# Streaming encoder trunk: the modulation's matmul groups of the first feed-forward, joined two by two

## The chip, the cores and the metric

The kernel runs on one core of a Trainium2 chip, in one launch. The core has five engines that work side by side, each from its own queue of instructions in a fixed order: TensorE (PE in the profile; its weight loads are listed apart as PEld), VectorE (DVE), ScalarE (ACT), GpSimd (POOL), and SyncE (SP), which here does nothing but issue DMA transfers. They wait for one another by semaphores. The metric is the device time of the whole launch in microseconds; lower is better.

## The reference, cut to what matters

An encoder with two layers works on 1024 prompt positions and 8 x 16 sample positions, 1152 rows of 1024 numbers in all. Every sub-layer is modulated by a conditioning vector `c`, of which there are nine (one for the prompt, eight for the samples):

```python
sc = jax.nn.silu(c)
for l in range(DEPTH):
    ada = (sc @ w_ada[l] + b_ada[l])[:, None, :]
    sh_m, sc_m, g_m, sh_f, sc_f, g_f = jnp.split(ada, 6, axis=-1)
    h = x * (1 + sc_m) + sh_m
    ...                                   # attention of the layer
    x = layer_norm(DEEPNORM_ALPHA * x + (1 + g_m) * mix, ...)
    h = x * (1 + sc_f) + sh_f
    f, conv_rows = conv_ffn(h, ..., w_up[l], conv_w[l], conv_b[l], w_down[l])
    x = layer_norm(DEEPNORM_ALPHA * x + (1 + g_f) * f, ...)
    if l == N_A_LAYERS - 1:
        ada_kv = (sc @ w_ada_kv + b_ada_kv)[:, None, :]
        ...                               # the K/V that the second layer uses
```

`conv_ffn` multiplies by `w_up` (1024 x 5632), runs a causal convolution of width 3 over the positions, gates one half by the other through a GELU, and multiplies by `w_down` (2816 x 1024). The modulation `sc @ w` is a product of nine rows with 1024 x 2048 numbers, seven times in all. It is small work, but its weights are 8 MB each time.

## The kernel before, in words

**Two streams of work.** TensorE does nearly everything that takes time. The modulation is computed beside it, in the background: `ada(gi, bank, ring)` (line 220) is a generator, and `step(n)` (line 200) pulls it on by one piece. Seven such pieces of modulation exist (`gi` 0 to 6). `gi` 0 is made in the opening, 1 and 2 run beside the first attention, and 3, 4, 5 and 6 run beside the first feed-forward: line 1422 queues them as `self.bg`.

**One modulation.** 1024 x 2048 weights come as 16 loads of 512 KB (line 229), for `k` of 0 to 7 (128 rows of the contraction) and `hf` of 0 and 1 (half of the columns). Each load feeds four matmuls (line 237): `cT`, 32 columns wide (nine used), is the stationary operand, and the array is used as four column tiles of 32, one per `j`, each with its own 256 moving columns. The type is fp32, for which every matmul leaves two records in the profile, so that one load's group is 8 records. All groups add up in one bank of PSUM (bank 7). Then a last piece adds the bias (`adab`, line 253), forms a gate row for two of the four (`gd`), turns the row with four transposes (line 264) and copies it to `adaT`. After each load's group, and after the last piece, the generator yields. `issue_after` ties a matmul behind another one in TensorE's queue; with `high_priority` this keeps the four matmuls of a load together.

**The first feed-forward.** The 22 column blocks of the gate's two halves are taken as pairs `j`. Pairs 0 and 1 are plain. Pairs 2 to 21 (`spair`, line 1389) use a scheme with seven products of half the size instead of eight (`products`, line 1154): the block of `w_up` for the one half is loaded into `sa`, that for the other into `sg`; GpSimd forms the sums S1, S2, S3 and `a21` from them (lines 1174 to 1177), each is split into a high and a low part (`split`, ScalarE then VectorE), and TensorE runs the products 11, 2, 21, 3, 1, 4, 22 in this order (pair 2: 11, 21, 22, 2, 3, 1, 4). Each is 24 matmuls (line 1226), 12 of 320 columns and 12 of 256. Product 11 and product 21 need only `sa`; product 2 needs S2, product 1 needs S1, and S1 = `a21` + `a22` is made of `sg`. Every product is read out of PSUM by `evict` before the next one adds to the same bank. The calls of line 1399 pull the background on by one piece after the first, third, fifth and seventh product: four groups of modulation per pair.

**The ring of slots.** `sa`, `sg`, every modulation load and the bias row all take the next slot of one ring of four, `wide` (line 1267): two slots of `ws` and two in `F`. A pair takes six of them, so a slot is reused four requests later, and a load can start only when the last reader of that slot is done. Line 1429 takes one more slot after pair 2 for `tables_b`, a small table; when that table is in `eb`, `skew_b` (line 1794) copies 384 KB of it in DRAM for each of 16 heads. These copies are written at pairs 3 to 18, but nothing ties them there but SyncE's queue.

**What sets the order.** The queues' orders are written by a planner when the program is built: it goes through the program with estimated times, and on each engine takes the instruction that stands first in the program among those that are ready by then. So a group of modulation can be moved a little ahead or back, and SyncE's queue can hold a copy ahead of a load that comes earlier in the program but whose slot was still taken.

Of the kernel before, what the change touches and what calls it, by code (L numbers as in the profile page):

```python
# [105 lines left out]
class Trunk:  # L106
# [110 lines left out]
                pass  # L217


    def ada(self, gi, bank, ring=None):  # L220

        nc = self.nc
        ring = ring or self.ws
        ps = self.bank(bank)
        lead = [None] * 4
        for k in range(8):
            for hf in range(2):
                w = ring.next()
                nc.sync.dma_start(w, self.I["adaw"][gi, k, hf])
                for j in range(4):  # L230
                    with ExitStack() as es:
                        if lead[j] is not None:
                            es.enter_context(self.tc.issue_after(lead[j]))
                        if j:
                            es.enter_context(self.tc.high_priority())
                            es.enter_context(self.tc.issue_after(first))
                        mm = nc.tensor.matmul(
                            ps[32 * j : 32 * j + 32, hf * 256 : hf * 256 + 256],
                            self.cT[:, k * 32 : k * 32 + 32],
                            w[:, j * 256 : j * 256 + 256],  # L240
                            start=k == 0 and hf == 0,
                            stop=k == 7 and hf == 1,
                            tile_position=(0, 32 * j),
                            skip_group_check=True,
                        )
                    first = mm.ins if j == 0 else first
                    lead[j] = lead[j] or mm.ins
                yield
        row = ring.next()
        bsrc = self.I["adab"][gi : gi + 1, :]  # L250
        for j in range(4):
            nc.sync.dma_start(
                row[32 * j : 32 * j + 32, 512:1024].rearrange("p (h x) -> p h x", h=2),
                bass.AP(bsrc.tensor, bsrc.offset + j * 256, [[0, 32], [1024, 2], [1, 256]]),
            )
        nc.vector.tensor_add(row[:, 0:512], ps, row[:, 512:1024])
        gate = {1: (0, 0), 2: (1, 1), 5: (2, 0), 6: (3, 1)}.get(gi)
        if gate is not None:
            g, hf = gate
            nc.gpsimd.tensor_scalar_add(row[:, 512:768], row[:, hf * 256 : hf * 256 + 256], 1.0)  # L260
            for j in range(4):
                nc.sync.dma_start(self.gd[g, :, j * 256 : j * 256 + 256], row[32 * j : 32 * j + 9, 512:768])
        for i in range(4):
            nc.tensor.transpose(ps[:, i * 128 : i * 128 + 128], row[:, i * 128 : i * 128 + 128], self.ident)
        dst = self.adaT[:, gi * 144 : gi * 144 + 144].rearrange("p (h j i r) -> p h i j r", h=2, j=4, i=2)
        src = ps.rearrange("p (h i j r) -> p h i j r", h=2, i=2, j=4)
        for h in range(2):
            nc.vector.tensor_copy(dst[:, h], src[:, h, :, :, 0:9])
        yield
# [971 lines left out]
    def ffn(self, l, xsrc, xdst, affs):  # L1241
        nc, I, O, H, F = self.nc, self.I, self.O, self.H, self.F
# [11 lines left out]
        g = nc.gpsimd  # L1254
# [12 lines left out]
        wide = Ring(self.ws.items + [F[:, 11644:12668], F[:, 8700:9724]])  # L1267
# [76 lines left out]
        def gated(j, ya, yg):  # L1344
            nc.scalar.activation(yg, yg, AF.Gelu_apprx_tanh)
            nc.gpsimd.tensor_mul(yg, yg, ya)  # L1346
            if l == 0 or j % 2:
                nc.sync.dma_start(self.actD[j], yg)
                if l:
                    self.pend.append(j // 2)  # L1350
            else:
                for r in (slice(0, 512), slice(1024, 1152)):
                    nc.sync.dma_start(self.actD[j][:, r], yg[:, r])

        def act_sums():
            for m in self.pend:
                a11, a21 = ygate[0][:, 0:512], ygate[0][:, 512:1024]
                a12, a22 = ygate[1][:, 0:512], ygate[1][:, 512:1024]
                nc.gpsimd.tensor_add(a22, a21, a22)
                nc.gpsimd.tensor_sub(a21, a11, a21)  # L1360
                nc.gpsimd.tensor_sub(a11, a22, a11)
                nc.gpsimd.tensor_sub(a12, a12, a11)
                for i in range(2):
                    nc.sync.dma_start(self.actS[m, i], ygate[i][:, 0:1024])
            self.pend = []

        def weight_sums(m):
            b11, b12, b21, b22 = (t[:, o : o + 512] for t in self.w0 for o in (0, 512))
            for i in range(2):
                nc.sync.dma_start(self.w0[i], I["wdn"][l, 2 * m + i])  # L1370
            nc.gpsimd.tensor_sub(b12, b22, b12)
            nc.gpsimd.tensor_add(b22, b12, b11)
            nc.gpsimd.tensor_sub(b21, b22, b21)
            nc.sync.dma_start(self.wT[m, 0][:, 512:1024], b12)
            nc.sync.dma_start(self.wT[m, 1], self.w0[1])
# [13 lines left out]
        def spair(j):  # L1389
            sa, sg = self.ws.next(), self.ws.next()  # L1390
            nc.sync.dma_start(sa, I["wup"][l, j])
            pairdma = nc.sync.dma_start(sg, I["wup"][l, j + 22]).ins
            ua, ug = us.next(), us.next()
            y = []
            row = conv_row_psum if l else conv_row

            def after(i, q):
                if i % 2 == 0:
                    self.step(1)
                if l and i == 1:  # L1400
                    act_sums()
                if l and i == 2 and j in wsum:
                    with self.tc.issue_after(pairdma):
                        weight_sums(wsum.index(j))
                if q == 4:
                    y.append(ygate[j % 2] if l else ys.next())
                    row(ug, j, 1, y[0])

            self.products(sa, sg, ua, ug, (S1, S2, S3), p1s, sub, TT, after, "first" if j == NPL else None)
            ya = yact if l else ys.next()  # L1410
            row(ua, j, 0, ya)
            gated(j, ya, y[0])
# [6 lines left out]
            self.take_w0(F32)  # L1419
        self.ws = wide  # L1420
        if l == 0:
            self.bg = [self.ada(g, 7, wide) for g in (3, 4, 5, 6)]
        self.tsums(Ring([F[:, 1536:2560], F[:, 8700:9724], F[:, 11644:12668]]), (0, 1, 2, 3, 4, 8, 5, 6, 7), T1S, TT)
        for u in us.items:
            nc.gpsimd.memset(u[:, 0:2], 0.0)
# [631 lines left out]
```

## Time and profile before

| what | value |
|---|---|
| time, median of 3 runs | 2776.96 us (2775.85 to 2781.15) |
| the profiled execution's own time | 2778.73 us |
| its span, first to last instruction | 2776.9 us |
| TensorE busy | 2656.2 us (96%) |
| VectorE, ScalarE, GpSimd busy | 69%, 49%, 38% |
| DMA queue of SyncE, share of 16 engines | 54.6% |
| pairs 2 to 21 of the first feed-forward on TensorE | 532.3 to 1036.1 us of the span |
| modulation groups of that stretch | 547.0 to 961.2 us, 512 records |

In the profile each line of an order of time has its start in us from the span's start, its length, engine, line of the kernel, operation, what it writes and reads, its shape and how many instructions were merged into it. Behind them, in brackets, stands how long the engine had stood idle before and what ended that. A busy TensorE is an engine with records on it; matmuls overlap, so that lengths can't be added, and distances from start to start are what counts.

### The profile page before, as it was taken

To read this page: it belongs to the slowest core of one execution; us is meant where nothing else is said; L and a number is where in the kernel's file an instruction comes from. 1 tells how busy PE (TensorE), PEld (TensorE's weight loads), DVE (VectorE), ACT (ScalarE), POOL (GpSimd) and SP (SyncE) were. 2 spreads that over 40 slices of the span, in tenths; PEclk is the share of its full clock that TensorE was granted. 3 is DMA by queue.
4 is the path that set the end of the run, shared out by engine and by line. 5 is a ranking of instruction groups with operands and counts; after the bars stand their busy time and mean duration, and the time that the engine had idled before them with its cause. 6 is when DMAs were issued, how large, how long until landed. Compare 5 with 4: busy or idle time off the path is not lost.

```text
span 2776.9 us, 47111 instructions
## 1 busy us (share of the span) xinstructions
PE 2656.2 (96%) x17266; PEld 2345.9 (84%) x17266; DVE 1916.0 (69%) x3836; ACT 1348.0 (49%) x2777; POOL 1065.7 (38%) x775
## 2 busy tenths in 40 slices
PE   7999889999999999999999999989999999999997
PEld 5987768989999998888898888867899999997776
DVE  4376767776666684767754667766787777785669
ACT  3475723433334343443536666662454445454454
POOL 3132623444434357664220121242466656632101
PEclk9999999999999999999999999989999999999999
DMA  7756434464444446765757457773544443347564
GB/s 289 236 162 193 145 103 167 163 236 148 139 158 147 147 135 220 240 217 182 277 192 263 121 155 195 213 213 115 176 143 173 144 138 135 136 148 246 189 221 155
DMA packets 229527, 498.27 MB, mean 179 GB/s; under 512 B 37456, under 2 KB 99232, under 8 KB 229296
## 3 DMA queue, kind: packets, MB, share of 16 engines
q1 hardware_dynamic: 229296, 495.27, 54.6%
q8 instruction: 136, 2.23, 0.3%
q14 instruction: 95, 0.78, 0.1%
HBM read 378.15 MB, written 126.47 MB: 182 GB/s over the span
## 4 chain that ended last, share of the span: by engine, by line
PE 38%; DVE 6%; DMA 4%; ACT 2%; issue 1%; POOL 0%; SPq 0%; DVEq 0%; ACTq 0%; POOLq 0%
PE PS L1226 18%; PE PS L1600 5%; PE PS L322 5%; PE PS L309 4%; PE PS L605 2%; PE PS L583 2%; DMA xa<-actD 1%; PE PS L554 1%; DVE xa L191 1%; DVE F L521 1%; DVE wl L191 1%; PE PS L557 1%; DMA xa<-actS 1%; PE PS L732 0%; DMA wl<-wT 0%
## 5 line engine op out<-in xcount | busy, mean ns | idle before, releaser
L1226 PE MATMUL PS<-H,wh 128*128 128x256 f32 (+1 forms) x2288 | 355.8, 296 | 0.0
L1187 DVE TENSOR_TENSOR F<-PS,F 128x256 f32<-128x256 f32 (+1 forms) x446 | 197.9, 453 | 182.1 <-PE PS L1226 172.7
L1226 PEld LDWEIGHTS PS<-H,wh 128*128 128x128 f32 x2288 | 322.6, 190 | 0.4 <-issue 0.4
L180 ACT CAST wh<-F 128x512 fp32r<-128x512 f32 (+3 forms) x241 | 147.7, 624 | 212.5 <-PE PS L1226 105.5
L191 DVE TENSOR_TENSOR wl<-F,wh 128x512 fp32r<-128x512 f32 (+2 forms) x225 | 213.4, 960 | 40.6 <-ACT wh L180 38.4
L1226 PE MATMUL PS<-H,wl 128*128 128x256 f32 (+1 forms) x1144 | 202.0, 297 | 6.2 <-ACT F L1194 6.2
L1600 PE MATMUL PS<-wh,xa 128*128 128x512 f32 x584 | 187.8, 398 | 14.6 <-ACT wh L180 7.6
L1226 PEld LDWEIGHTS PS<-H,wl 128*128 128x128 f32 x1144 | 168.6, 189 | 12.1 <-ACT F L1194 6.4
L1226 PE MATMUL PS<-xa,wh 128*128 128x320 f32 (+1 forms) x1152 | 175.2, 293 | 0.0
L180 ACT CAST xa<-xa 128x384 fp32r<-128x384 f32 (+2 forms) x143 | 85.8, 604 | 176.0 <-DMA xa<-actD 149.6
L1226 PEld LDWEIGHTS PS<-xa,wh 128*128 128x128 f32 x1152 | 159.0, 188 | 0.4 <-issue 0.4
L1469 DVE TENSOR_TENSOR xa<-xa 128x384 fp32r<-128x384 f32 x66 | 94.4, 1441 | 83.4 <-ACT xa L180 83.3
L1600 PEld LDWEIGHTS PS<-wh,xa 128*128 128x128 f32 x584 | 110.3, 190 | 44.3 <-ACT wh L180 11.8
L180 ACT CAST wh<-ws 128x512 fp32r<-128x512 f32 (+1 forms) x131 | 95.5, 736 | 101.4 <-PE PS L1226 44.2
L643 POOL TENSOR_TENSOR F<-F,x2r 64x512 f32<-64x512 f32 x62 | 79.4, 1280 | 165.9 <-DVE F L619 149.3
L1346 POOL TENSOR_TENSOR F<-F 128x1152 f32<-128x1152 f32 x44 | 124.1, 2820 | 43.9 <-DVE F L1339 18.1
L322 PE MATMUL PS<-xa,H 128*128 128x512 f32 x504 | 133.5, 406 | 6.2 <-ACT xa L180 3.3
L309 PE MATMUL PS<-H,w0r 128*128 128x384 f32 (+1 forms) x720 | 136.1, 340 | 0.0
L1275 DVE SCALAR_TENSOR_TENSOR F<-F 128x1024 f32<-128x1024 f32 (+2 forms) x160 | 132.1, 876 | 3.1 <-ACT F L1314 2.1
L309 PE MATMUL PS<-H,wh 128*128 128x384 f32 (+1 forms) x672 | 131.1, 338 | 0.0
L583 PE MATMUL PS<-C,F 128*128 128x128 f32 x720 | 112.7, 281 | 14.5 <-DVE wh L590 5.8
L309 PEld LDWEIGHTS PS<-H,w0r 128*128 128x128 f32 x720 | 123.2, 188 | 2.8 <-issue 1.1
(354 smaller groups left out, 6883.8 us busy)
## 6 DMA issues: line engine op xcount, KB each, us to landing
ws<-in_adaw_dram SPq DMA_DIRECT2D x64, 512.0 KB
ws<-in_wup_dram SPq DMA_DIRECT2D x49, 512.0 KB
F<-in_adaw_dram SPq DMA_DIRECT2D x48, 512.0 KB
F<-in_wup_dram SPq DMA_DIRECT2D x39, 512.0 KB
actD<-F SPq DMA_DIRECT2D x33, 576.0 KB
ws<-in_wdn_dram SPq DMA_DIRECT2D x33, 512.0 KB
F<-in_wdn_dram SPq DMA_DIRECT2D x33, 512.0 KB
xa<-kH SPq DMA_DIRECT2D x60, 256.0 KB
```

The source lines that it names most:

```text
L180: nc.scalar.copy(out, in_)
L191: self.eng(el).tensor_sub(lo, src, hi.bitcast(F32))
L309: mm = self.nc.tensor.matmul(out[:, 0:n], w[a][:, k * 128 : k * 128 + 128], H[:, p, k, s0 : s0 + n], start=i == 0, stop=i == 23)
L322: self.nc.tensor.matmul(out[:, 0:n], H[:, p, j * kn + k, t0 : t0 + 128], w[a][:, k * n : k * n + n], start=i == 0, stop=i == 23,)
L583: nc.tensor.transpose(t[:, n * 128 : n * 128 + 128], p[:, (kt - k0) * 128 : (kt - k0) * 128 + 128], self.ident)
L643: self.eng("v" if last else "p").tensor_mul(on[r, q], on[r, q], rb[r, :])
L1187: nc.vector.tensor_add(d, v(ps), a if len(a.shape) == 3 else v(a))
L1226: self.pairmm = nc.tensor.matmul(ps[:, 0:m], w[a][:, k * 128 : k * 128 + 128], x(p, k, n), start=start and c == 0, stop=c == 11, skip_grou ...
L1275: nc.vector.scalar_tensor_tensor(o, u, cw[:, cc, i : i + 1], o, op0=ALU.mult, op1=ALU.add)
L1346: nc.gpsimd.tensor_mul(yg, yg, ya)
L1469: nc.vector.tensor_sub(lo, raw, hi.bitcast(F32))
L1600: self.downmm = nc.tensor.matmul(ps, a[p][:, i * 128 : i * 128 + 128], w[q], start=first and c == 0, stop=last and c == 2, skip_group_chec ...
```

## The change

`ada` gets a parameter `per`, the number of loads that make one piece. With `per` of 1 it does what it did before, and so it stays beside the first attention. Beside the first feed-forward `per` is 2: a piece issues the loads of `hf` 0 and 1 of one `k`, then the matmuls of `hf` 1, then those of `hf` 0, and all but the first of these eight matmuls are tied behind the first at high priority. The generator has nine pieces instead of seventeen. They are pulled on after the third and the seventh product of a pair, and no longer after the first, third, fifth and seventh. Four modulations are then 36 pieces in 18 pairs; before they were 68 pieces in 17 pairs.

```diff
-    def ada(self, gi, bank, ring=None):
+    def ada(self, gi, bank, ring=None, per=1):
...
-        for k in range(8):
-            for hf in range(2):
-                w = ring.next()
-                nc.sync.dma_start(w, self.I["adaw"][gi, k, hf])
+        order = [(k, hf) for k in range(8) for hf in range(2)]
+        for o in range(0, 16, per):
+            loads = []
+            for k, hf in order[o : o + per]:
+                loads.append(ring.next())
+                nc.sync.dma_start(loads[-1], self.I["adaw"][gi, k, hf])
+            first = None
+            for (k, hf), w in reversed(list(zip(order[o : o + per], loads))):
                 for j in range(4):
                     with ExitStack() as es:
                         if lead[j] is not None:
                             es.enter_context(self.tc.issue_after(lead[j]))
-                        if j:
+                        if first is not None:
                             es.enter_context(self.tc.high_priority())
                             es.enter_context(self.tc.issue_after(first))
...
-                            start=k == 0 and hf == 0,
-                            stop=k == 7 and hf == 1,
+                            start=o == 0 and lead[j] is None,
+                            stop=o + per == 16 and hf == (0 if per > 1 else 1),
...
-                    first = mm.ins if j == 0 else first
+                    first = first or mm.ins
                     lead[j] = lead[j] or mm.ins
-                yield
+            yield
...
             def after(i, q):
-                if i % 2 == 0:
+                if i in (2, 6):
                     self.step(1)
...
-            self.bg = [self.ada(g, 7, wide) for g in (3, 4, 5, 6)]
+            self.bg = [self.ada(g, 7, wide, 2) for g in (3, 4, 5, 6)]
```

## The prediction

> **What bounds the kernel now.** I read the page first, then the first feed-forward by stretches, then TensorE's order of work there, then the queue that issues the loads.
>
> ```profile
> span 2776.9 us, 47111 instructions
> PE 2656.2 (96%) x17266; PEld 2345.9 (84%) x17266; DVE 1916.0 (69%) x3836; ACT 1348.0 (49%) x2777; POOL 1065.7 (38%) x775
> ```
>
> ```profile
> 532.30:561.10 28.80, 26.38 (x202) 24.33 (x200) 19.95 (x38) 12.27 (x23) 10.63 (x11) 0.94 0.52 162
> 561.10:616.80 55.70, 50.80 (x405) 46.40 (x402) 40.88 (x54) 19.93 (x35) 21.43 (x15) 1.00 0.72 251
> 616.80:968.50 351.70, 351.70 (x2786) 323.34 (x2785) 234.28 (x362) 133.78 (x225) 143.45 (x108) 1.00 0.44 146
> 968.50:1036.10 67.60, 67.00 (x507) 66.75 (x506) 56.94 (x77) 32.52 (x53) 36.31 (x23) 1.00 0.39 127
> ```
>
> The stretches (columns: PE, PEld, DVE, ACT, POOL busy, then clock, DMA share, GB/s) are pair 2; pairs 3 and 4; pairs 5 to 18; and 19 to 21. From pair 5 on TensorE is busy for 351.70 of 351.70 us at a granted clock of 1.00, DVE for two thirds of it and the DMA engines for 0.44. There only TensorE's own time counts, so a shorter record stream is time won. Pairs 3 and 4 are another stage: 4.9 us of TensorE idle, DMA at 0.72.
>
> **What a switch to the modulation's records costs.** TensorE's order of time, in four places: a period of four groups, seven products without any group, and the two places where two groups already stand together.
>
> ```profile
> 546.44 0.60 PE L1226 MATMUL PS<-xa,wh 128*128 128x320 f32 x3
> 546.98 1.07 PE L237 MATMUL PS<-F,C 128*32 128x256 f32 x16
> 547.98 1.00 PE L1226 MATMUL PS<-xa,wh 128*128 128x320 f32 x5
> ...
> 576.56 0.64 PE L237 MATMUL PS<-ws,C 128*32 128x256 f32 x8 [1.77 <-DMA ws<-in_adaw_dram]
> 577.02 0.61 PE L237 MATMUL PS<-F,C 128*32 128x256 f32 x8
> 577.56 1.29 PE L1226 MATMUL PS<-H,wh 128*128 128x320 f32 x7
> ...
> 720.50 0.64 PE L237 MATMUL PS<-ws,C 128*32 128x256 f32 x8
> 721.07 0.85 PE L1226 MATMUL PS<-xa,wl 128*128 128x320 f32 x4
> ...
> 745.68 0.64 PE L237 MATMUL PS<-F,C 128*32 128x256 f32 x8
> ...
> 978.16 0.75 PE L1226 MATMUL PS<-xa,wl 128*128 128x320 f32 x4
> ...
> 1000.31 0.75 PE L1226 MATMUL PS<-H,wl 128*128 128x320 f32 x4
> ```
>
> Seven products take 1000.31 - 978.16 = 22.15 us (3.16 each). The same seven with four groups take 745.68 - 720.50 = 25.18. So a group of eight records costs (25.18 - 22.15) / 4 = 0.76 us. Only 0.57 of it (721.07 - 720.50) lies from its first record to the next product; the other 0.19 is lost to the products at its two edges, as the first four records behind it show (0.85 against the usual 0.75). Sixteen records together take 547.98 - 546.98 = 1.00 and 577.56 - 576.56 = 1.00: the second eight add 0.43. Joining two groups therefore saves 0.76 - 0.43 = 0.33 us.
>
> ```profile
> L237 PE MATMUL PS<-ws,C 128*32 128x256 f32 x208 | 16.6, 391 | 0.0
> L237 PE MATMUL PS<-F,C 128*32 128x256 f32 x208 | 16.6, 391 | 0.0
> ```
>
> Pairs 5 to 18 hold 416 records, 52 groups, which become 26: **26 x 0.33 = 8.6 us less**. Nothing else is removed: the same 64 loads, the same records. The bounds: if the two joined rows above are flattered by their places, and a join saves only one of the two edges, half of it, 4.3; upwards, the whole stretch has (351.7 - 14 x 22.15) / 52 = 0.80 per group, three closing rows included, and 26 x 0.37 makes 9.6. I take 8.6, since both joined rows agree to 0.01.
>
> A rule speaks against this. The Trainium skill, page "TensorE: Matmul & The Clock Gate", Part 3, "What overlaps and what doesn't", says that a weight load overlaps running matmuls only where the row group differs; these tiles differ by column only. By it the second eight records would show their eight weight loads in the open; by the joined rows of this trace (0.43 us for the second eight) they do not.
>
> **What the move does to the loads.** Products go by their names here (P11, P2, P21, P3, P1, P4, P22, in this order within a pair) and their places by first to seventh. In pairs 5 to 18 the ring of four slots mostly works out so: a pair's own two weight loads (`sa`, `sg`) reuse the slots of the first two modulation loads of the pair before. Today these are free after its first and its third product, in the change both after the third; `sa` is issued some 7 us later (now 721.21, then beside 728.31) and `sg` a few tenths later.
>
> ```profile
> 717.26 0.33 SPq L229 DMA_DIRECT2D F<-in_adaw_dram  x1
> 721.21 0.33 SPq L1391 DMA_DIRECT2D ws<-in_wup_dram  x1
> 725.27 0.33 SPq L1348 DMA_DIRECT2D actD<-F  x1
> 728.31 0.33 SPq L1392 DMA_DIRECT2D F<-in_wup_dram  x1
> ```
>
> ```profile
> 731.79 1.29 POOL L1174 TENSOR_TENSOR F<-F 128x512 f32<-128x512 f32 x1 [6.54 <-DMA F<-in_wup_dram]
> 733.04 1.29 POOL L1176 TENSOR_TENSOR F<-ws,F 128x512 f32<-128x512 f32 x1
> ```
>
> A load takes 3.5 us (728.31 to the sum that waited for it, 731.79). Two behind each other: some 5.5. `S2` (line 1176) is then there 2 us later than now, at 736.3. P2, which needs it, is the second product of the next pair: this pair starts one product before the group at 720.50, at 717.3, the next some 24.5 us later, its P2 at 745. That cover of nearly 9 us, less 3 for the split, holds. What queues behind the two loads on SyncE is the `actD` store and the next modulation loads; POOL waits 2 us longer at `S1` (it idles 6.54 there), and nothing but the `actD` store waits for it. The two loads of the group behind the third product are issued at the pair's start, when the last group of the pair before frees their slots, and have 3 x 3.16 = 9.5 us for 5.5. So I cost the steady pairs at nothing; without that cover each missing microsecond comes 14 times.
>
> **The one place where the slot counts: pair 3.** Line 1429 takes one slot after pair 2, so pair 3's `sg` reuses the slot of pair 2's third modulation load. Its records run at 550.27 now; in the change they come behind the seventh product, with the fourth load's, at 560.54.
>
> ```profile
> 550.27 0.64 PE L237 MATMUL PS<-ws,C 128*32 128x256 f32 x8
> ...
> 560.54 0.64 PE L237 MATMUL PS<-ws,C 128*32 128x256 f32 x8
> 561.11 0.85 PE L1226 MATMUL PS<-H,wl 128*128 128x320 f32 x4
> ...
> 619.85 0.64 PE L237 MATMUL PS<-ws,C 128*32 128x256 f32 x8
> ```
>
> ```profile
> 551.00 0.59 SPq L1392 DMA_DIRECT2D ws<-in_wup_dram  x1
> 554.00 0.33 SPq L229 DMA_DIRECT2D F<-in_adaw_dram  x1
> 554.39 8.59 SPq L1794 DMA_DIRECT2D skb<-eb  x10
> ...
> 566.16 0.33 SPq L229 DMA_DIRECT2D ws<-in_adaw_dram  x1
> ...
> 571.05 3.82 SPq L1794 DMA_DIRECT2D skb<-eb  x3
> ...
> 577.72 0.39 SPq L1392 DMA_DIRECT2D F<-in_wup_dram  x1
> ```
>
> ```profile
> 555.26 1.30 POOL L1174 TENSOR_TENSOR F<-ws 128x512 f32<-128x512 f32 x1 [6.48 <-DMA ws<-in_wup_dram]
> ...
> 588.61 1.26 POOL L1174 TENSOR_TENSOR F<-F 128x512 f32<-128x512 f32 x1 [14.72 <-DMA F<-in_wup_dram]
> ```
>
> ```profile
> 558.29 1.77 DVE L191 TENSOR_TENSOR wl<-F,wh 128x512 fp32r<-128x512 f32 x1
> ```
>
> Today that load goes out at 551.00, ahead of the sixteen copies of line 1794, and lands in 4.3 us (555.26). In the change it is free at about 561 and goes out behind some ten copies, at about 563. Its flight there is between 4.3 us and the 10.4 of the load at 566.16 (its records start at 576.56) or 10.9 (577.72 to 588.61); I take 8.5, nearer the crowded rows: it lands at 571.5. From landing to the end of `S2`'s split took 560.06 - 555.26 = 4.8, so P2 can start at 576.3. P11 and P21 need `sa` alone; they fill 560.8 (561.11 less 0.33) to 567.1. TensorE then idles up to 9.2 us, and some 2.6 less if P1, which needs only `S1` (one POOL sum and the wait for it earlier, 1.3 each), goes first. I take 8.
>
> Pair 5 starts one product before 619.85, at 616.7. In the change it starts at 560.8 + 14 products (44.3) + four joined groups (4 x 1.19 = 4.8) + 8 = 617.9: **1.2 us more**. The present waits in that stretch (4.9 us) are gone in this count, since they too were for loads that the new stall lets land.
>
> **Sum:** -8.6 + 1.2 = -7.4 us. The profiled execution took 2778.73 us, 1.8 above its span and 1.8 above the median shown (2776.96). 2778.73 - 7.4 = 2771.3; against the median, **2769.5**.
>
> **Rivals.**
> (a) *Pair 3 is not held up*: the planner puts pair 2's last sixteen records early (it used one group to fill a gap at 550.27), or the load ahead of the copies. For it: 550.27 was such a gap. Against: in the change P1 stands before them in the program and has no wait there. Pair 5 then starts at 609.9 plus the 1.8 us wait of 576.56, 611.7: -5.0 - 8.6 = -13.6, 2763.4.
> (b) *Slower: pair 3 is held up in full.* If `sg` goes out behind all sixteen copies (they end at 574.9, row 571.05), with 10.9 us it lands at 586, P2 starts at 591, the idle time is 24 us: +17.2 - 8.6 = +8.6, 2785.5. It decides from an idle time of 15.4 us, a landing after 577.8. Against: in the program `sg` comes ahead of every copy, so the planner holds it back only while its slot is taken.
> (c) *The steady pairs wait for their paired loads*: 0.6 us in each of 14 pairs takes all 8.6 away: about 2777. Against it is the 4 us of cover above; for it, that the first record of sixteen now needs the second load.
> (d) *The sixteen do not run as one*: if the second eight show their eight weight loads, a join costs more than the switch it saves.
>
> ```profile
> L237 PEld LDWEIGHTS PS<-ws,C x256: 106/108/109, 550.3 to 961.2; 128*32 128x32 f32 x128
> ```
>
> At 0.108 each that is 0.86 + 0.43 = 1.29 against 0.76, +0.53 for each of 26, and 0.86 more for each of the four in pairs 3 and 4: 13.8 + 3.4 + 1.2 = 18.4 more, 2795.4. The two rows of sixteen speak plainly against it. By the rule of the Trainium skill above ("TensorE: Matmul & The Clock Gate", Part 3) this is what would happen.
>
> **How the numbers follow.** Forecast 0.47, (a) 0.23, (b) 0.10, (c) 0.16, (d) 0.02, and 0.02 for the rest. About 0.2% (5.6 us) is what a measurement of this kernel can tell from no change, so faster means below 2771.4. The forecast's own range, from a stall of 5 to 12 us and 8.6 +-1, is 2765.5 to 2774.5; some two thirds of it is faster. With (a) and a little of (c): faster 0.57, within 0.2% 0.31, slower 0.12. The range takes in most of (a) and (c): 2762 to 2779.
>
> **What would show it.** In TensorE's order of time of the changed kernel: 32 rows of sixteen records, each about 1.00 us to the next product, two in a pair; a period of 22.15 + 2 x 1.19 = 24.5 us instead of 25.2; an idle time of 6 to 9 us in pair 3, put down to DVE or ACT, behind two products on `H`; SyncE issuing pair 3's second weight load after 561 and not at 551. A wait ahead of line 237's first record in pair after pair would mean (c), a pair 3 without idle time (a). I am wrong in the main term if a period is not 0.6 to 0.7 us shorter.

## The result

The changed kernel takes **2792.18 us** (median), the kernel before 2776.38 us beside it: a ratio of **1.0058, with a 95% interval of 1.0038 to 1.0077**. It is slower by about 16 us. The forecast was 2769.5 us, and the range ended at 2779.

The profiled execution is the median one. First the two head lines of its page, then its first feed-forward by stretches (columns as before: length, then PE, PEld, DVE, ACT and POOL busy, clock, DMA share, GB/s). Line numbers have moved: the products are line 1230 (1226 before), the modulation's matmuls 241 (237), VectorE's evictions 1191 (1187), and the loads of `sa` and `sg` 1395 and 1396 (1391 and 1392).

```profile
span 2790.4 us, 47111 instructions
PE 2660.4 (95%) x17266; PEld 2353.0 (84%) x17266; DVE 1929.2 (69%) x3836; ACT 1346.1 (48%) x2777; POOL 1068.0 (38%) x775
```

```profile
531.20:618.10 86.90, 77.33 (x603) 72.04 (x601) 58.35 (x90) 31.21 (x56) 29.75 (x25) 0.96 0.59 201
618.10:977.70 359.60, 349.69 (x2768) 326.26 (x2764) 238.90 (x362) 132.44 (x225) 141.95 (x107) 1.00 0.40 140
977.70:1051.80 74.10, 69.75 (x529) 67.93 (x526) 56.39 (x79) 33.21 (x55) 37.46 (x24) 1.00 0.43 147
```

The instructions are the same in number, and no engine is noticeably busier. The stretches are pairs 2 to 4, 5 to 18 and 19 to 21. They took 84.5, 351.7 and 67.6 us before and take 86.9, 359.6 and 74.1 now: +2.4, +7.9 and +6.5, together 16.8 us. The second feed-forward is as long as it was (459.7 us before, 459.6 now), so the loss lies in the stage that was changed. Pairs 5 to 18, where TensorE was busy for every microsecond, now have 9.9 us without a record.

**What the joined groups cost.** TensorE's order of time in pair 9, which starts at 720.09:

```profile
719.09 1.07 PE L241 MATMUL PS<-ws,C 128*32 128x256 f32 x16
720.09 3.45 PE L1230 MATMUL PS<-H,w0r 128*128 128x320 f32 x24
...
737.24 0.76 PE L1230 MATMUL PS<-x2r,wl 128*128 128x320 f32 x4
737.84 1.33 PE L1230 MATMUL PS<-x2r,wh 128*128 128x320 f32 x8
739.01 0.63 PE L1230 MATMUL PS<-x2r,wl 128*128 128x256 f32 x4
...
740.40 0.85 PE L1230 MATMUL PS<-H,wl 128*128 128x320 f32 x4
741.10 1.34 PE L1230 MATMUL PS<-H,wh 128*128 128x320 f32 x8
742.63 0.74 PE L1230 MATMUL PS<-H,wl 128*128 128x256 f32 x4 [0.20 <-DVE F L1191]
743.21 1.11 PE L1230 MATMUL PS<-H,wh 128*128 128x256 f32 x8
744.26 1.07 PE L241 MATMUL PS<-F,C 128*32 128x256 f32 x16
```

Sixteen records take 720.09 - 719.09 = 1.00 us, as forecast. But the period is 744.26 - 719.09 = 25.17, not 24.5. The profile lists only 0.20 us of idle time, ahead of the last product's second half. The distance tells more: 742.63 - 741.10 = 1.53 us, where the same eight records of the product before take 739.01 - 737.84 = 1.17; the four ahead of them take 0.70 against 0.60. Ends of matmuls are modelled, so a wait shows more fully from start to start.

**Who makes it wait.** The waits of TensorE in pairs 5 to 18, and from there to the end of the stage (what it waited for, us in total, times, longest):

```profile
PE PS L1230 <- DVE F L1191: 9.0, 17, 1.9
PE PS L1230 <- ACT F L1198: 0.8, 1, 0.8
```

```profile
PE PS L1230 <- DVE F L1191: 3.4, 2, 2.5
PE PS L1230 <- ACT F L1198: 0.8, 1, 0.8
```

All of them are evictions; TensorE waits for the bank of PSUM to be read, not once for a split weight or for a modulation load. So the question is why VectorE evicts late. Its order of time in pair 9 of the kernel before (pair from 717.1):

```profile
725.20 0.69 DVE L191 TENSOR_TENSOR w0r<-ws,w0r 128x512 fp32r<-128x512 f32 x1 [0.20 <-ACT w0r L180]
725.81 0.69 DVE L191 TENSOR_TENSOR wl<-ws,wh 128x512 fp32r<-128x512 f32 x1
...
733.76 1.11 DVE L191 TENSOR_TENSOR wl<-F,wh 128x512 fp32r<-128x512 f32 x1 [1.75 <-ACT wh L180]
...
736.49 0.41 DVE L1187 TENSOR_TENSOR F<-PS,F 128x256 f32<-128x256 f32 x1
```

and of the changed kernel (pair from 720.1):

```profile
737.00 1.24 DVE L191 TENSOR_TENSOR wl<-F,wh 128x512 fp32r<-128x512 f32 x1 [2.33 <-ACT wh L180]
738.17 1.78 DVE L191 TENSOR_TENSOR w0r<-ws,w0r 128x512 fp32r<-128x512 f32 x1
...
740.27 1.37 DVE L191 TENSOR_TENSOR wl<-ws,wh 128x512 fp32r<-128x512 f32 x1
741.56 0.68 DVE L191 TENSOR_TENSOR w0r<-F,w0r 128x512 fp32r<-128x512 f32 x1
742.16 0.41 DVE L1191 TENSOR_TENSOR F<-PS,F 128x256 f32<-128x256 f32 x1
742.50 0.68 DVE L191 TENSOR_TENSOR wl<-ws,wh 128x512 fp32r<-128x512 f32 x1
```

A pair's loads make seven splits on VectorE. Before, the two of `sa` began at 8.1 us of the pair and the burst of the other five at 16.7. Now all seven come in one burst from 16.9 on. The eviction of product 1's second half stands behind four of them in VectorE's fixed order, and no longer behind two: it starts 22.1 us into the pair instead of 19.4, and the last product's second half, which needs its bank, starts when it is done (742.57). At the same time that last product has moved forward, since the group that stood behind product 1 (0.76 us) is gone. The burst is also longer than its number of splits says: the first three take 1.24, 1.78 and 1.37 us, the fourth 0.68. In pairs 5 to 18 of this kernel the 48 splits that overlap GpSimd's work take 1.46 us on average, the other 51 take 0.68, and here GpSimd forms its sums from 735.02 to 741.09.

The two splits are late because `sa` is. SyncE's and GpSimd's orders of time:

```profile
720.45 0.86 SPq L231 DMA_DIRECT2D ws<-in_adaw_dram  x2
730.02 0.33 SPq L1352 DMA_DIRECT2D actD<-F  x1
730.50 0.33 SPq L1396 DMA_DIRECT2D ws<-in_wup_dram  x1
730.93 0.84 SPq L1395 DMA_DIRECT2D ws<-in_wup_dram  x1
```

```profile
735.02 1.30 POOL L1178 TENSOR_TENSOR F<-ws 128x512 f32<-128x512 f32 x1 [5.03 <-DMA ws<-in_wup_dram]
```

Both slots come free with the joined group behind the third product, so `sg` (1396) and `sa` (1395) go out together, 10.4 and 10.8 us into the pair; before, `sa` went out 4.1 us into it (721.21) and `sg` 11.2 (728.31).

### The profile page after: what moved, and what is told of

It is laid out like the page before. It is cut to its first block, busy times and chain, and to the rows that moved or that the text cites. A ratio compares the mean times of both kernels' runs of the same rounds, so it can differ in the third digit from the quotient of the medians.

```text
span 2790.4 us, 47111 instructions
## 1 busy us (share of the span) xinstructions
PE 2660.4 (95%) x17266; PEld 2353.0 (84%) x17266; DVE 1929.2 (69%) x3836; ACT 1346.1 (48%) x2777; POOL 1068.0 (38%) x775
## 4 chain that ended last, share of the span: by engine, by line
PE 62%; DVE 13%; DMA 12%; issue 5%; ACT 4%; POOL 3%; SPq 1%; DVEq 0%; POOLq 0%; ACTq 0%
PE PS L1230 20%; PE PS L326 10%; PE PS L1480 9%; PE PS L313 7%; PE PS L1604 5%; DVE wl L191 3%; PE PS L609 2%; PE PS L587 2%; DMA ws<-in_wup_dram 2%; PE PS L241 1%; PE PS L558 1%; DMA F<-in_wup_dram 1%; PE PS L300 1%; DVE F L1191 1%; DVE F L525 1%
## 5 line engine op out<-in xcount | busy, mean ns | idle before, releaser
L1230 PE MATMUL PS<-H,wh 128*128 128x256 f32 (+1 forms) x2288 | 357.6, 298 | 0.0
L1279 DVE SCALAR_TENSOR_TENSOR F<-F 128x1024 f32<-128x1024 f32 (+2 forms) x160 | 129.3, 857 | 11.2 <-ACT F L1318 8.7
L180 ACT CAST wh<-ws 128x512 fp32r<-128x512 f32 (+1 forms) x132 | 96.1, 735 | 74.2 <-PE PS L1230 26.7
```

What stands on the lines that cost most here:

```text
L180: nc.scalar.copy(out, in_)
L1230: self.pairmm = nc.tensor.matmul(ps[:, 0:m], w[a][:, k * 128 : k * 128 + 128], x(p, k, n), start=start and c == 0, stop=c == 11, skip_grou ...
L1279: nc.vector.scalar_tensor_tensor(o, u, cw[:, cc, i : i + 1], o, op0=ALU.mult, op1=ALU.add)
```

## The experiments

The reading above leaves two things to tell apart: the **late loads**, which push seven splits into one burst, and the **missing cover**, the groups that used to stand between a product's eviction and the next use of its bank. Whether the join itself is worth 0.33 us is a third question, and pair 3 a fourth. One table for all kernels; the first column of numbers is the ratio to the kernel before with its interval, then pairs 5 to 18 from start to start, the idle time listed there, and pair 3. Stretches come from one profiled execution each, which is not always near the median: 2794.4 us against a median of 2786.1 for kernel 4, 2790.6 against 2782.0 for kernel 7, 2789.2 against 2803.4 for kernel 9, 2775.2 against 2766.9 for kernel 10.

| kernel | ratio | pairs 5-18, us | idle, us | pair 3, us |
|---|---|---|---|---|
| before | 1 | 351.7 | 0.0 | 29.3 |
| the change | 1.0058 [1.0038, 1.0077] | 359.6 | 9.8 | 33.5 |
| 1 `split_rings` | 1.0040 [1.0027, 1.0052] | 345.9 | 2.7 | 25.4 |
| 2 `own_ring` | 0.9990 [0.9976, 1.0004] | 346.2 | 3.1 | 25.4 |
| 3 `own_ring_four` | 0.9995 [0.9986, 1.0004] | 356.5 | 2.5 | 26.7 |
| 4 `late_loads_four` | 1.0055 [1.0036, 1.0075] | 349.5 | 0.7 | 36.4 |
| 5 `together_four` | 1.0038 [1.0024, 1.0051] | 356.6 | 2.5 | 31.0 |
| 6 `pull_first_fifth` | 0.9998 [0.9981, 1.0016] | 342.5 | 0.0 | 26.0 |
| 7 `two_steps_untied` | 1.0037 [1.0021, 1.0053] | 351.6 | 5.3 | 33.5 |
| 8 `cover_back` | 1.0077 [1.0053, 1.0100] | 356.4 | 2.1 | 38.3 |
| 9 `table_early` | 1.0104 [1.0078, 1.0129] | 357.6 | 7.7 | 25.1 |
| 10 `own_ring_row` | 0.9977 [0.9963, 0.9991] | 347.3 | 2.7 | 25.4 |

### 1. The changed kernel with rings of their own, in both layers

```diff
-        wide = Ring(self.ws.items + [F[:, 11644:12668], F[:, 8700:9724]])
+        wide = Ring(self.ws.items)
+        back = Ring([F[:, 11644:12668], F[:, 8700:9724]])
...
-            self.bg = [self.ada(g, 7, wide, 2) for g in (3, 4, 5, 6)]
+            self.bg = [self.ada(g, 7, back, 2) for g in (3, 4, 5, 6)]
```

> The change with one thing undone: the pair's own two weight loads have a ring of two slots to themselves (the ws slots), the modulation's loads and the bias row another (the two slots in F), so that a pair's weight loads no longer wait for a modulation group. Groups stay joined, sixteen records behind the third and the seventh product. Theory 1 (the change is slow because the pair's loads come late and together, their seven splits then fall in one burst on VectorE in front of the last evictions, and TensorE waits for these): the waits of TensorE on VectorE's eviction in pairs 5 to 21 go from some 13 us to under 2, the period comes to 24.5 us, pair 3 no longer waits; 5 to 12 us faster than the kernel before. Rival 2 (the single groups between the products were the cover of the evictions, and the loads do not matter): the waits stay, 8 to 18 us slower than before.

Measured: the first feed-forward is some 6 us shorter than before (528.7 to 1026.0, against 532.3 to 1036.0), with steady periods of 24.6 us and no idle time in pair 3. The whole launch is slower by 0.40%, because the second feed-forward, where nothing was meant to change, takes 476 us instead of 460: its ring too was cut, from four slots to two. What follows: with the weights' loads freed from the modulation the changed stage is faster than before; the edit was too wide.

### 2. The same in the first layer alone

```diff
+        slots = [F[:, 11644:12668], F[:, 8700:9724]]
+        wide = Ring(self.ws.items + (slots if l else []))
+        back = Ring(slots)
...
+            self.bg = [self.ada(g, 7, back, 2) for g in (3, 4, 5, 6)]
```

> The change with the pair's weight loads on a ring of their own, as in the run with separate rings, but in the first feed-forward alone; the second keeps its ring of four, which that run had cut to two (its second feed-forward took 476 us against 460). Theory 1, mended (the joined groups save 0.33 us each, and the loss comes from late weight loads): the first feed-forward ends some 10 us earlier than before, as there (1026 against 1036), and now the rest keeps it: 6 to 12 us faster than before. If what was lost behind has another cause: no faster than before.

Measured: 2770.86 against 2772.88 us, less than the 6 to 12 us expected, and by the interval not clear of no change. In the first feed-forward the steady period is 24.6 us; the second is normal again (461.7). The stretch of pairs 5 to 18, and TensorE's waits in it:

```profile
612.90:959.10 346.20, 343.09 (x2769) 324.33 (x2765) 288.41 (x360) 134.15 (x224) 150.36 (x107) 1.00 0.41 146
```

```profile
PE PS L1230 <- DVE F L1191: 3.1, 3, 2.2
```

Here VectorE is busy for 288.4 us where the changed kernel has 238.9, with as many instructions, and yet TensorE waits for it in 3 places and not in 17. So it was not how much VectorE has to do but **in what order**. `sa` does not go out earlier than in the change (12.9 us into the pair, where the change has 10.8 and the kernel before 4.1). But `sg` now follows 9 us behind it, at 21.9, and the splits are spread over the pair. It is the burst that is gone, not the lateness. The waits that are left are in pairs 6, 10, 15 and 19, those that end a modulation. The largest stand behind one instruction of VectorE, the bias sum, which waits for a load of the bias row:

```profile
980.59 0.69 DVE L260 TENSOR_TENSOR F<-PS,F 128x512 f32<-128x512 f32 x1 [5.95 <-DMA F<-in_adab_dram]
```

### 3. Own rings without the join

```diff
+            self.bg = [self.ada(g, 7, back) for g in (3, 4, 5, 6)]
```

(the rings as in 2, on the kernel before).

> The kernel before with the same two rings in the first feed-forward, four single groups per pair, nothing joined. It prices the join alone against the run own_ring. Theory 1: a period of 25.2 us as before, pairs 3 and 4 some 2 to 6 us shorter, so 0 to 6 us faster than before and 6 to 12 us slower than own_ring. If the ring and not the join is what own_ring gains by: as fast as own_ring.

Measured: the period is the old one, 25.18 us for four groups; with the join and the same rings it is 24.59. That is (25.18 - 24.59) / 2 = **0.30 us per join**, against 0.33 forecast. So the gain is the join's and not the rings'. (That the stretch is longer than before is mostly one pair, 29.1 us, in which the first matmuls of a new modulation wait 2.5 us for VectorE to copy out the last one.) Of whole launches these two can't be told apart (0.9990 and 0.9995, with intervals that overlap). In the profiled executions the stage is 6.4 us shorter with the join, but it starts 3.6 us later (533.0 against 529.4); why no more than 1.1 us is left between the medians is not shown.

### 4. Late loads with four groups

The kernel before, with one slot of the ring passed over in each pair, so that a pair's loads wait for other groups than they did.

```diff
                 if i % 2 == 0:
                     self.step(1)
+                if l == 0 and i == 6:
+                    self.ws.next()
```

> The kernel before, four single groups per pair, with one slot of the ring passed over in each pair, so that a pair's first weight load waits for the group behind the third product of the pair before and its second for the one behind the fifth (before: first and third). Nothing is joined. Theory 1 (late loads make the burst of splits): TensorE waits on VectorE's eviction in most pairs, 10 to 30 us slower than before. Rival 2 (lost cover between products): the four groups are all there, so no waits, within 3 us of before.

Measured: the expectation of waits in every pair failed. The steady pairs hardly wait (0.7 us in 14 pairs). What was lost lies in pairs 3 and 19 (9.6 and 6.3 us of idle time). In this kernel the two loads go out one at a time: `sa` 5 to 14 us into the pair, `sg` at about 18, 4 to 13 us apart. All the groups are there, one of them behind product 1 in nearly every pair; fifteen times two of them stand together as sixteen records, and so the stretch is even shorter than before. A later load by itself is therefore not the cause.

### 5. Both loads together, with four groups

The kernel before; in the first layer `sg` goes out first and `sa` right behind it, as in the changed kernel.

```diff
-            nc.sync.dma_start(sa, I["wup"][l, j])
+            if l:
+                nc.sync.dma_start(sa, I["wup"][l, j])
             pairdma = nc.sync.dma_start(sg, I["wup"][l, j + 22]).ins
+            if l == 0:
+                with self.tc.issue_after(pairdma):
+                    nc.sync.dma_start(sa, I["wup"][l, j])
```

> The kernel before, four single groups per pair, with the pair's first weight load issued right behind its second, so that both come behind the group after the third product, as in the change. Theory 1 in its plain form (late and together is enough for the burst of seven splits to delay the evictions): TensorE waits on VectorE in most of pairs 5 to 18, together over 6 us, 6 to 15 us slower than before. Theory 4 (it takes both: the burst, and no group between product 1 and product 22 to cover the late eviction): under 2 us of waits in pairs 5 to 18; within 5 us of before.

Measured, pairs 5 to 18:

```profile
PE PS L1226 <- DVE F L1187: 2.5, 4, 1.2
```

The burst alone brings the waits back, but few: 4 instead of 17, +4.9 us on 351.7. It is neither nothing nor the whole.

### 6. The change, pulled after the first and the fifth product

```diff
-                if i in (2, 6):
+                if i in (0, 4):
```

> The change with the joined groups pulled on behind the first and the fifth product in place of the third and the seventh. The pair's weight loads then find their slots free after the first product, and one group stands again between product 1 and product 22. Theory 1: both weight loads come some 6 us earlier than in the change, no burst at the end of the pair, few waits; 4 to 10 us faster than before. Rival 2: also faster, as the cover is back between the fifth and the sixth product; so this run does not tell the two apart, but shows whether joining pays. If neither holds: as slow as the change.

This kernel forms other sums in the modulation than the reference, with the same instructions; only its time is read. Why its sums differ is not known, so its time is a support here and not a price. Measured: 342.5 us for pairs 5 to 18, without any idle time. The forecast's sum for them was 351.7 - 8.6 = 343.1 with 26 joined groups in them; with the 25 that fall into them here, its prices give 341.9 (the working stands below). Here one joined group stands behind product 1, where the changed kernel has none, and the other frees two slots early in the pair: the two loads go out together, but 4.0 and 4.4 us into it. Of the 9.2 us gained, 2.7 were lost in pairs 2 to 4 (pairs 2 and 4 idle 4.3 and 4.0 us) and 1.9 in pairs 19 to 21, and the whole launch is no faster (0.9998).

### 7. Two single pieces per pull, not tied

The kernel before, with the change's places alone.

```diff
-                if i % 2 == 0:
-                    self.step(1)
+                if i in (2, 6):
+                    self.step(2)
```

> The kernel before with two pieces of modulation pulled on behind the third and the seventh product, one load each, and no tie between the two groups of a pair. Slots and loads as in the change. If where the pieces are pulled on is to blame (theory 1 or rival 2): as slow as the change, 8 to 18 us slower than before. Rival 3 (the tie that keeps sixteen records together holds up the products behind it): as fast as before or a few us faster.

Measured: pairs 5 to 18 as long as before (351.6), with 5.3 us of idle time in them. The stage starts 4.5 us later (536.8), and pair 5 at 625.8 instead of 616.8, so the opening differs as well. In pairs 5 to 18 both of the things to be told apart are there: the two loads go out late and together (in most pairs some 11.5 and 12 us into the pair, `sa` first), and no group stands behind product 1. The groups stand together even without the tie, 24 times as sixteen records. By the forecast's prices that makes 351.7 - 24 x 0.33 = 343.8 us, so 7.8 are lost, where the change loses 17.7 (worked out below). And the waits are others; here are those of these pairs:

```profile
PE PS L1226 <- ACT F L1194: 4.6, 9, 1.0
PE PS L237 <- issue: 0.7, 1, 0.7
```

They are for ScalarE's evictions, ahead of the third product, and not one is for VectorE. In pair 13 (from 850.4) the eviction of product 1's second half stands behind three splits, starts 20.9 us into the pair, and nothing waits for it:

```profile
871.27 0.41 DVE L1187 TENSOR_TENSOR F<-PS,F 128x256 f32<-128x256 f32 x1
```

So late loads and missing cover together do not yet make VectorE's evictions late. This kernel differs from the change in the tie and in the order of the two loads, and with them in VectorE's order; no run changes one of these alone.

### 8. The change, with cover behind product 1

Four matmuls on resident data (`cT` by `cT`) into bank 6, tied behind product 1 of every pair. This adds work that nobody reads.

```diff
+                if l == 0 and i == 4:
+                    first = None
+                    for c in range(4):
...
+                            mm = nc.tensor.matmul(
+                                self.bank(6)[32 * c : 32 * c + 32, 0:256],
+                                self.cT[:, 0:32],
+                                self.cT[:, 0:256],
```

> The change with four idle matmuls more in every pair, on resident operands and into a bank that nobody reads, tied behind product 1, where the kernel before had a group: 0.76 us of TensorE's time per pair that does nothing but stand between product 1 and the products behind it. Theory 4 (the waits need both the burst of splits and the missing group there): the waits on VectorE in pairs 5 to 21 fall from 12.4 us to under 4, so that 20 x 0.76 = 15 us of added work cost less than 8 us; the time stays within 8 us of the change. Theory 1 in its plain form (the burst alone): the waits stay near 12 us and the kernel is some 15 us slower than the change.

Measured, pairs 5 to 18:

```profile
623.40:979.80 356.40, 354.25 (x2881) 327.61 (x2877) 238.57 (x360) 132.28 (x225) 141.77 (x107) 1.00 0.40 141
```

```profile
PE PS L1230 <- DVE F L1191: 1.2, 2, 1.1
PE PS L1230 <- ACT F L1198: 0.9, 1, 0.9
```

The stretch has 112 more records, 14 groups at 0.76 us, 10.6 us of added work, and is 3.2 us **shorter** than in the change. So the added group takes 10.6 + 3.2 = 13.8 us of loss out of it. The launch as a whole is no faster, since pair 3 happened to idle 10.4 us here, 6.5 of it for a modulation load.

### 9. The table taken before the stage

```diff
+        if l == 0:
+            self.tables_b(self.ws.next())
         for j in range(NPL):
             plain(j)
...
-            if l == 0 and j == 2:
-                self.tables_b(self.ws.next())
```

(on the changed kernel).

> The change with the small table taken from the ring ahead of pair 0 and not behind pair 2, so that it no longer shifts the ring: pair 3's second weight load then reuses a slot freed in the middle of pair 2, and the table's sixteen copies no longer stand before it. Prices pair 3's part of the loss. All theories of the steady pairs: pair 3's wait of 6.7 us is gone (25 us and not 33.5), the waits on VectorE in pairs 5 to 21 stay; 5 to 10 us faster than the change, still 2 to 10 us slower than before.

Measured: pair 3's stall is gone (25.1 us, no idle time), so it did come from the slot that the table takes. But the kernel is the slowest of all. The copies of `skb` now run at 395.6 to 411.4 us, before the stage; the stage starts at 539.5 instead of 531.2, and pair 2 idles 6.9 us. That the copies cause this is not shown, and the profiled execution, the fastest of the four, does not show where the others lose 12 to 21 us more. The steady waits are what they were (7.7 us), so they do not depend on pair 3.

### 10. Own rings, and the bias row earlier in the program

```diff
-            yield
+            if per == 1 or o + per < 16:
+                yield
         row = ring.next()
...
+        if per > 1:
+            yield
         nc.vector.tensor_add(row[:, 0:512], ps, row[:, 512:1024])
```

(on kernel 2).

> own_ring with the bias row of each modulation loaded one piece earlier, together with its last pair of groups. In own_ring VectorE stood still for 5.95 us at the last modulation's addition, waiting for this load, and TensorE waited behind it in four pairs (0.33, 2.25, 0.53 and 2.15 us). If that is all: those waits go, 3 to 5 us faster than own_ring, 5 to 9 us faster than the kernel before (ratio 0.997 to 0.998), pairs 5 to 18 in 344.5 us against 351.7. If the row's load is not what VectorE waits for: as own_ring.

Measured: 2766.88 against 2773.01 us, **0.9977 [0.9963, 0.9991]**, the one kernel of the eleven whose interval lies below 1, and so faster than the kernel before, by 0.23%. The expected reason isn't seen, though. VectorE still stands at the bias sum:

```profile
755.73 0.69 DVE L263 TENSOR_TENSOR F<-PS,F 128x512 f32<-128x512 f32 x1 [5.74 <-DMA F<-in_adab_dram]
```

and TensorE's idle time in pairs 5 to 18 is 2.7 us against 3.1; but this execution is the slowest of its twelve. By the code the row takes a slot of a ring of two, which the last group's matmuls hold wherever the row's load stands in the program; no run tried it with a slot of its own. Whether this kernel is really faster than kernel 2 stays open: their intervals overlap.

## Why the prediction was wrong

**The price of a join was right.** 0.33 us was forecast, 0.30 measured (kernels 2 and 3), and where nothing waits the steady pairs take 342.5 us (kernel 6) against 341.9 by the forecast's prices. Rival (d) is refuted by the rows of sixteen records, 1.00 us each, where it had 0.57 + 1.29 = 1.86. The rule of the Trainium skill cited with it ("TensorE: Matmul & The Clock Gate", Part 3, "What overlaps and what doesn't") does not describe these column tiles.

**The step that failed is "So I cost the steady pairs at nothing".** The cover that I counted was for the load, the sums and the split of S2 up to product 2, and it held: no wait for a split appears in pairs 5 to 18. What I had noted as "`sa` is issued some 7 us later" came true, and I followed it only to the product that needs it. Two things were left out. The splits of `sa` are instructions in VectorE's queue, and moved by 7 us they land in the burst of the other five, ahead of an eviction that has nothing to do with them. Kernels 2 and 4 show that in the steady pairs the delay as such does no harm: it is the burst. With it goes a wrong reading: I had written that nothing but the `actD` store waits for GpSimd's first sum, but a split waits for it as well (in the kernel before VectorE's at 733.76, behind ScalarE's part of it). And the groups taken out were themselves the cover for evictions: 0.76 us of records that need nothing from VectorE, behind the first and the fifth product. I counted the removed group as time saved and not as slack removed.

How much each is worth, in pairs 5 to 18. 25 joined groups fell into them (the 26th into pair 19; 400 records instead of 416), so by the forecast's prices they should take 351.7 - 25 x 0.33, less the two groups that left the stretch, 2 x 0.76: 341.9 us. The change takes 17.7 more. Loads apart, cover still missing (kernel 2): 4.3 more, most of it the bias row. Loads late, cover back (kernel 8): 356.4 - 341.9 - 10.6 = 3.9 more. Loads together, cover never removed (kernel 5): 4.9 more than before. So each half alone costs up to 5 us and both together 17.7: **the loss of the change needs both**. They are not enough by themselves, though. Kernel 7 has both, loses 7.8 us, and waits for VectorE nowhere in these pairs; there the eviction stands behind three splits and not four. Whether the tie or the order of the two loads puts the fourth ahead of it stays open.

**Behind pair 18** I counted nothing, and 6.5 us were lost. 1.6 of it is the last joined group and closing piece, now in pair 19 (23.87 us instead of 22.28). 4.5 is pair 20 (26.76 instead of 22.22): no group is left there to lengthen the pair, but its loads still went out together behind pair 19's, and the evictions waited 3.3 us.

**Pair 3 came as told, by luck in part.** Pair 5 starts at 618.1; 617.9 was forecast. The rows of pair 3:

```profile
566.40 0.64 PE L241 MATMUL PS<-ws,C 128*32 128x256 f32 x8 [1.66 <-DMA ws<-in_adaw_dram]
...
573.69 1.43 PE L1230 MATMUL PS<-H,wl 128*128 128x320 f32 x4 [5.09 <-DVE wl L191]
574.92 2.33 PE L1230 MATMUL PS<-H,wh 128*128 128x320 f32 x8
...
579.61 3.45 PE L1230 MATMUL PS<-xa,w0r 128*128 128x320 f32 x24
```

```profile
558.67 0.58 SPq L1396 DMA_DIRECT2D ws<-in_wup_dram  x1
559.30 10.45 SPq L1798 DMA_DIRECT2D skb<-eb  x9
```

```profile
567.68 1.29 POOL L1178 TENSOR_TENSOR F<-ws 128x512 f32<-128x512 f32 x1 [8.80 <-DMA ws<-in_wup_dram]
```

`sg` went out at 558.67, behind five copies and not ten, and landed 9.0 us later (8.5 estimated). The idle time is 5.09 + 1.66 = 6.75 us against 8. Against that stand 2.8 us that I had not counted, since the product after the stall took 579.61 - 573.69 = 5.92 us instead of 3.16; and the whole stage began 1.1 us earlier.

**The rivals.** (a) is refuted: pair 3 was held up. (b) had the right sign from the wrong place; `sg` was never held behind all sixteen copies. (c) had the right shape, a wait in pair after pair (0.2 to 2.4 us listed in 11 of the 14), but its mechanism is absent: no wait stands ahead of line 241 in pairs 5 to 18. (Its time also left out the 1.2 us of pair 3, which make it about 2778 and not 2777.) The case that came true, late evictions, was not among the rivals.

## What the runs showed of the clock

I had counted a stall at its idle time. It can cost more. Pair 11 of the changed kernel, TensorE's order of time and the windows around it:

```profile
791.13 1.33 PE L1230 MATMUL PS<-H,wh 128*128 128x320 f32 x8
794.36 0.83 PE L1230 MATMUL PS<-H,wl 128*128 128x256 f32 x4 [1.90 <-DVE F L1191]
794.99 1.91 PE L1230 MATMUL PS<-H,wh 128*128 128x256 f32 x8
796.83 1.08 PE L241 MATMUL PS<-F,C 128*32 128x256 f32 x8
```

```profile
793.00:796.00 3.00, 1.64 (x9) 1.64 (x10) 3.00 (x7) 0.47 (x1) 0.00 (x0) 0.81 0.48 161
796.00:800.00 4.00, 4.00 (x31) 2.69 (x30) 3.58 (x7) 1.83 (x3) 0.22 (x1) 0.72 0.48 162
800.00:806.00 6.00, 6.00 (x48) 6.00 (x47) 4.78 (x8) 2.81 (x5) 2.98 (x2) 1.00 0.46 161
...
573.00:576.00 3.00, 2.31 (x9) 2.31 (x10) 3.00 (x3) 1.62 (x4) 2.92 (x3) 0.50 1.09 314
```

After 1.90 us of idle time the granted clock fell to 0.81 and 0.72 in the next two windows and was back at 1.00 from 800. Eight records took 796.83 - 794.99 = 1.84 us, where the same eight take 744.26 - 743.21 = 1.05 in pair 9. Behind the 5.09 us of pair 3 it was 0.50. Pair 11 is 29.37 us long; of the 4.8 over a period of 24.6 its listed idle time explains 2.33. From the last product's second half to the next pair it took 798.51 - 794.36 = 4.15 us, in pair 9 745.26 - 742.63 = 2.63: that is 1.5 us more for the slower clock. But not every such stall does this: in pair 20 TensorE waited 2.48 us ahead of 1021.88, and all windows from 1018 to 1026 show 1.00. What decides between the two is not shown. The Trainium skill, page "TensorE: Matmul & The Clock Gate", Part 1, "What's actually happening", says that the clock falls to half after an idle window of about 3.4 us. The 0.50 in pair 3 agrees; in pair 11 it fell after a shorter stall.

Also unexpected: with the modulation on a ring of its own, VectorE's same 360 instructions take 288 us instead of 239, whether the groups are joined or not. The traces show where they do. VectorE's and GpSimd's work overlap for 162 us of kernel 2's pairs 5 to 18, for 97 of the changed kernel's, and only what overlaps has become longer. In kernel 2 a split takes 0.69 us alone and 1.77 beside GpSimd, a multiply-add of 128x112 takes 0.32 and 0.87, while an eviction of 128x256 out of PSUM takes 0.41 or 0.42 either way.

## What to carry to other kernels

Filler work on the bottleneck engine is also slack for whoever must clear its buffers: before joining or removing it, look at what is evicted behind it, and with how much to spare. When a change delays a load, follow every instruction that hangs on the load into its engine's queue, and ask what stands behind it there, not only whether the load's own consumer is in time. An engine two thirds busy can be late in most periods if its work comes in one burst, the more so where another engine slows that work down. And a stall of 2 us on TensorE can cost 1.5 us more in clock, as in pair 11, or nothing, as in pair 20.
